# Token-major u, q and k blocks, dense attention in three queued steps, later state-space groups and decay rows sent by DMA, in a two-layer hybrid trunk

## The chip, the cores and the metric

The kernel runs on one core of one Trainium2 chip. The metric is the device time of one execution in microseconds; the time before is the median of three runs. The profile is of one execution. In it TensorE is PE, its weight loads PEld, VectorE DVE, ScalarE ACT, GpSimd POOL, and SyncE, which issues nearly all DMAs, SP.

## What is computed

A trunk of two layers on 256 tokens of width 2048, all in float32, with modulation by a conditioning vector (adaLN). Layer 0 mixes with a spatial-gating MLP (A) beside a state-space scan (B), layer 1 with stick-breaking attention (C, 12 heads of 128) beside dense softmax attention (D, 4 heads; with 256 tokens the block-sparse choice has one block, the token's own). Each layer ends with a SwiGLU FFN. Cut to what the change touches:

```python
# layer 0
u, v, z, xbc, dt_raw = split(hm @ w_in)
v  = layer_norm(gelu(v))                       # in chunks of 128 tokens, heads of 128 columns
mixed = einsum('hts,bcshe->bcthe', tril(w_s), v) + b_s.T[:, :, None]
y_a = gelu(u) * mixed
x, B, C = split(silu(conv(xbc)));  dt = softplus(dt_raw + bias)
a_cum = cumsum(dt * a)                         # per head, in chunks of 128 tokens
y   = (tril(C B^T) * exp(a_cum_t - a_cum_s)) (x dt) + C state exp(a_cum) + d * x
y_b = rms_norm(y * silu(z))
x   = x + gate * (concat(y_a, y_b) @ w_out)
# layer 1
qc, kc, vc, qd, kd, vd = split(hm @ w_in)
y_c = stick_breaking(qc, kc, vc)               # sigmoid weights, cumulated backwards over the keys
y_d = softmax(rms(qd) rms(kd)^T / sqrt(128), causal) vd
x   = x + gate * (concat(y_c, y_d) @ w_out)
```

## The kernel before

**Products.** A weight is taken in slabs of 256 rows by 512 columns (`wslab`, L323): one DMA of 512 KB into `raw` (4 buffers), a cast on ACT to `hi` in fp32r (L331), the rest on DVE to `lo` (L336), 3 buffers each. Every product is three fp32r products: hi by hi, hi by lo, lo by hi. There are two forms of a block of 512 output columns. `dense_ws` (L361) keeps the weight in the array and lets the 256 tokens pass: 8 slabs x 2 x 3 x 4 = 192 matmuls of 256 columns (L379), with the result feature by token. `dense_as` (L399) keeps the activation in the array and lets 512 weight columns pass: 96 matmuls of 512 columns (through `mm`, L163), with the result token by feature. An accumulator takes half of the four PSUM banks of pool psA (2 buffers); everything else uses `pm()`, 4 banks, and smaller tiles with few buffers each (`t2` and `t1` 6, `xc` 3).

**Order.** The program is unrolled, and a list scheduler orders each engine's instructions by priority (place in the program, moved forward by `high_priority`), by its own estimate of time, and by free buffers; each engine then runs its list in that order. `later` holds work that `dense_as` and `dense_ws` issue behind the third slab of the next block (DEFER = 6 k-tiles), `preps` holds steps of which one is issued ahead of each slab, `pump` spreads the adaLN products (L208 on DVE, fed by `araw` DMAs) over the slabs.

**Layer 0.** 14 blocks in ORDER (x, v, z) are made in three passes over k. Then come the 4 u blocks in `dense_ws`, then the output projection in two halves of 4 blocks each: the ya half (k-tiles of y_a), then the yb half (k-tiles of y_b). After u, 16 splits (`split`, L468 to 470) make the pairs of y_a from `vt`, which holds v, then mixed, then y_a, with the columns on partitions after `spatial`. The pairs lie in the same slots (`hslot`) as those of the norm's output that the u blocks read.

**State-space groups.** `ssd_group(g)` works on 4 k-tiles. For each k-tile j it spreads two rows of the cumulated decay over 128 partitions by four small matmuls (identR by `ath` and `atl`, result `bc` in a `pm` bank), makes the decay matrix on ACT (L897, L899, L904) and DVE (L900, L905), multiplies on PE into `py`, and adds on DVE (L913). `ssd_out` then multiplies by z (L971) and sums squares (L498). The four groups stand behind blocks SSD_AT = (12, 14, 16, 18) of the running count: 12 is z2, 14 and 16 are the blocks u0 and u2, 18 is the first block of the ya half. The splits of y_b are L1230 and L1231.

**Layer 1.** vd in `dense_as`, then qd and kd in `dense_ws`; `rstd_of` forms each head's root mean square by a product with ones (8 in all) and L482, L1351. Dense attention runs head by head (L1363 to L1388). Then for each of three groups of four heads: q and k blocks in `dense_ws`, the weights w of the stick-breaking heads (L1401 to 1421, two `t2` tiles and one `pm` bank a head), a v block in `dense_as`, and the products with v (`y_out` splits them, L469 and L470). The output projection takes the k-tiles in the order 12 to 15, then 0 to 11.

Of the kernel before, what the change touches and what calls it, by code (L numbers as in the profile page):

```python
# [8 lines left out]
F32 = mybir.dt.float32  # L9
F32R = mybir.dt.float32r  # L10
# [5 lines left out]
P = 128  # L16
# [34 lines left out]
SSD_AT = (12, 14, 16, 18)  # L51
# [3 lines left out]
def trunk(ctx: ExitStack, tc: tile.TileContext, x, c, norm_mix_g, norm_ffn_g, ada_w, ada_b,  # L55
# [69 lines left out]
    identR = cst.tile([HB, HB], F32R, name="identR")  # L125
    V.tensor_copy(identR, ident[0:HB, 0:HB])
# [4 lines left out]
    def small_loads():  # L131

        for dst, src in ((rows2[0:96, :], ssd_conv_w[0].rearrange("j (k p) -> (j k) p", p=P)),
# [6 lines left out]
                         (rows1[82:83, 0:HB], ssd_d),  # L140
                         (hb[:, 0, :], ssd_dt_bias.partition_broadcast(P)),
# [218 lines left out]

    def dense_ws(w, c0, ks, ahead=W_AHEAD):  # L361
# [38 lines left out]
    def dense_as(w, c0, ks, ahead=W_AHEAD, head=None, tail=False, hold=False):  # L400
# [13 lines left out]
        for pi, part in enumerate(parts):  # L414
# [15 lines left out]
            for n, j, (r, i, x) in order:  # L430
# [5 lines left out]
                bh, bl = run[i][1]  # L436
# [37 lines left out]

    def rstd_of(sqs, scale):

        ps = pm()
        for i, t in enumerate(sqs):
            mm(ps[:, 0:S], ones, t, first=(i == 0), last=(i == len(sqs) - 1))
        r = tmp.tile([P, S], F32, tag="rb", name="rb", bufs=2)  # L480
        A.activation(r, ps[:, 0:S], AF.Sqrt, bias=eps6, scale=scale)
        V.reciprocal(r, r)  # L482
        return r
# [300 lines left out]
    ath = st([HB, S], "ath", F32R)  # L784
    atl = st([HB, S], "atl", F32R)
# [3 lines left out]
    def ssd_dt():  # L789
# [48 lines left out]
        A.activation(ath, psat[0:HB, 0:S], AF.Copy)  # L838
        V.tensor_tensor(atl, psat[0:HB, 0:S], ath.bitcast(F32), op=OP.subtract)
# [3 lines left out]
        V.tensor_copy(dcol, psD[:, 0:KT])  # L843

# [10 lines left out]
    def ssd_group(g):  # L855
# [29 lines left out]
        for j in range(4):  # L885
            kt = 4 * g + j
            bc = pm()
            for i in range(2):
                h = 2 * kt + i
                oh = identR[:, h:h + 1].to_broadcast([HB, P])  # L890
                mm(bc[:, i * S:(i + 1) * S], oh, ath, first=(i == 0), last=False)
                mm(bc[:, i * S:(i + 1) * S], oh, atl, first=False)
# [11 lines left out]
            A.activation(cev, bc.rearrange("p (i t) -> p i t", i=2)[:, :, P:S], AF.Exp)  # L904
            V.tensor_tensor(cev, cev, cT[:, None, P:S].to_broadcast([P, 2, P]), op=OP.mult)  # L905
# [37 lines left out]
    def mix(b, h):  # L943
        return vt[b][:, :, h * P:(h + 1) * P]

    def spatial(b):
# [8 lines left out]
        bs = t2().rearrange("p (h t) -> p h t", h=4)  # L955
        nc.sync.dma_start(bs, gm_b_s[:, 4 * b:4 * b + 4, :].partition_broadcast(P))
        for h2 in range(2):
            ps = pm()
            for i in range(2):
                h = 2 * h2 + i  # L960
                for cc in range(2):
                    o = i * S + cc * P
                    mm(ps[:, o:o + P], mix(b, h)[:, cc, :], w[:, h, :], first=(i == 0 and cc == 0))
            for i in range(2):
                h = 2 * h2 + i
                V.tensor_tensor(mix(b, h), ps[:, i * S:(i + 1) * S].rearrange("p (c t) -> p c t", c=2),
                                bs[:, h, None, :].to_broadcast([P, 2, P]), op=OP.add)
# [39 lines left out]
    rate[0] = RATE  # L1007
    for b in range(4):
# [333 lines left out]
    for c0, gcol in ((QD0, 80), (KD0, 81)):  # L1342
        acc = dense_ws(w_in1, c0, ks1)
        t = b4()
        with tc.high_priority(offset=600):
            A.activation(t, acc, AF.Copy)
# [128 lines left out]
```

## Time and profile before

| | |
|---|---|
| median of 3 runs | 2578.42 us (2578.0 to 2580.18) |
| time of the profiled execution | 2575.71 us |
| its span, first to last instruction | 2574.0 us |
| mean granted TensorE clock | 0.999 |
| PE / PEld / DVE / ACT busy | 99% / 85% / 73% / 49% |
| DMA | 672.96 MB, mean 261 GB/s |

PE is busy for 99% of the span, but matmuls are pipelined and overlap in the records, so the busy share doesn't say how much of it is needed. The chain of work in order of time gives, for each run of matmuls of one kind, its length and its count; their quotient is the spacing of the matmuls, and that is what the engine's time is made of.

### The profile page before, as it was taken

Reading aid. Unit: us, or ns where it says so; the run is one execution under the profiler, and the core shown is the slowest. Engines: PE = TensorE matmul, PEld = TensorE weight load, DVE = VectorE, ACT = ScalarE, POOL = GpSimd, SP = SyncE. Lnnn points to the kernel's source line nnn. Section 1 sums busy time; section 2 is a strip of 40 time slices with the busy share of each in tenths; the row PEclk is TensorE's granted clock in tenths of the full one; section 3 lists DMA queues with packets and bytes.
Section 4 is the critical chain, followed back from the end, with each engine's and each line's share of the span. In section 5 each row is a group of like instructions: output and inputs, shape, how many; then the busy total and the mean of one; then the engine's idle time right before and its main releaser. Section 6 shows DMA issues by size and latency. Waiting matters only on the chain.

```text
span 2574.0 us, 35773 instructions
## 1 busy us (share of the span) xinstructions
PE 2542.3 (99%) x13621; PEld 2184.9 (85%) x13621; DVE 1876.0 (73%) x2027; ACT 1263.5 (49%) x1612; POOL 5.4 (0%) x19
## 2 busy tenths in 40 slices
PE   7999999999999999999999999999999999999999
PEld 6999899988788888888888899998788888888887
DVE  7899887889878888777777787768765455545454
ACT  5535866645645443344444655544744443344443
POOL 0000000000000000000000000000000000000000
PEclk9999999999999999999999999999999999999999
DMA  9999667798799988998998688888686666666655
GB/s 347 313 347 310 196 207 239 259 310 296 266 326 331 312 302 313 322 315 302 307 305 304 216 269 265 257 265 284 196 266 195 190 188 203 199 193 190 188 202 166
DMA packets 307830, 672.96 MB, mean 261 GB/s; under 512 B 24048, under 2 KB 26570, under 8 KB 307658
## 3 DMA queue, kind: packets, MB, share of 16 engines
q1 hardware_dynamic: 307530, 670.66, 79.1%
q8 instruction: 106, 1.74, 0.3%
q14 instruction: 66, 0.54, 0.1%
q10 hardware_dynamic: 128, 0.02, 0.0%
HBM read 668.46 MB, written 2.13 MB: 261 GB/s over the span
## 4 chain that ended last, share of the span: by engine, by line
PE 96%; DVE 1%; ACT 1%; DMA 1%; issue 0%; SPq 0%; ACTq 0%; DVEq 0%
PE accps L163 69%; PE accps L379 19%; PE pm L163 7%; PE pm L154 1%; DVE acc L208 1%; DMA blk<-in_ada_w 0%; DMA raw<-in_ffn_w_gate 0%; DMA t<-in_gm_w_s 0%; PE pm L871 0%; DMA t<-in_gm_ln_b 0%; DVE t L1134 0%; ACT h L1130 0%; DVE xr L1037 0%; ACT t L927 0%; ACT t L1121 0%
## 5 line engine op out<-in xcount | busy, mean ns | idle before, releaser
L331 ACT ACTIVATE hi<-raw 128x1024 fp32r<-128x1024 f32 (+1 forms) x864 | 903.1, 1046 | 1168.8 <-PE accps L163 880.7
L336 DVE TENSOR_TENSOR lo<-raw,hi 128x1024 fp32r<-128x1024 f32 (+1 forms) x864 | 1039.5, 1205 | 566.5 <-ACT hi L331 560.7
L163 PE MATMUL accps<-hi,h 128*128 128x512 f32 x1840 | 498.0, 391 | 0.0
L163 PE MATMUL accps<-lo,h 128*128 128x512 f32 x1840 | 494.6, 390 | 0.0
L163 PE MATMUL accps<-hi,l 128*128 128x512 f32 x1840 | 494.0, 390 | 0.0
L208 DVE SCALAR_TENSOR_TENSOR acc<-araw,ct,acc 128x1024 f32<-128x1024 f32 (+2 forms) x377 | 465.5, 1235 | 3.5 <-DMA araw<-in_ada_w 3.0
L163 PEld LDWEIGHTS accps<-hi,l 128*128 128x128 f32 x1840 | 344.9, 188 | 72.0 <-issue 0.2
L163 PEld LDWEIGHTS accps<-lo,h 128*128 128x128 f32 x1840 | 344.2, 188 | 71.8
L163 PEld LDWEIGHTS accps<-hi,h 128*128 128x128 f32 x1840 | 341.7, 188 | 68.6 <-ACT hi L331 0.2
L379 PE MATMUL accps<-h,hi 128*128 128x256 f32 x1392 | 376.5, 285 | 2.5 <-ACT h L522 1.7
L379 PE MATMUL accps<-h,lo 128*128 128x256 f32 x1392 | 376.1, 285 | 1.3 <-DVE lo L336 1.3
L379 PE MATMUL accps<-l,hi 128*128 128x256 f32 x1392 | 374.6, 285 | 0.0
L163 PE MATMUL accps<-hi,blk 128*128 128x512 f32 x1440 | 357.5, 390 | 0.0
L163 PEld LDWEIGHTS accps<-hi,blk 128*128 128x128 f32 x1440 | 269.5, 188 | 55.6
L379 PEld LDWEIGHTS accps<-h,hi 128*128 128x128 f32 x1392 | 259.3, 192 | 5.3 <-ACT h L522 1.9
L379 PEld LDWEIGHTS accps<-h,lo 128*128 128x128 f32 x1392 | 258.7, 192 | 2.7 <-DVE lo L336 1.5
L379 PEld LDWEIGHTS accps<-l,hi 128*128 128x128 f32 x1392 | 258.8, 192 | 0.8
L163 PE MATMUL accps<-lo,blk 128*128 128x512 f32 x720 | 192.5, 389 | 0.0
L163 PEld LDWEIGHTS accps<-lo,blk 128*128 128x128 f32 x720 | 135.1, 188 | 28.1
L163 PE MATMUL pm<-hi,blk 128*128 128x512 f32 x224 | 57.0, 390 | 0.3 <-ACT hi L331 0.3
L579 DVE TENSOR_TENSOR blk<-accps,blk 128x1024 f32<-128x1024 f32 x40 | 48.7, 1218 | 3.1 <-PE accps L163 2.6
L163 PEld LDWEIGHTS pm<-hi,blk 128*128 128x128 f32 x224 | 42.0, 188 | 9.4 <-ACT hi L331 0.7
(282 smaller groups left out, 1335.8 us busy)
## 6 DMA issues: line engine op xcount, KB each, us to landing
araw<-in_ada_w SPq DMA_DIRECT2D x323, 512.0 KB, 5.6
raw<-in_ffn_w_gate SPq DMA_DIRECT2D x176, 512.0 KB, 4.5
raw<-in_ffn_w_up SPq DMA_DIRECT2D x176, 512.0 KB, 4.4
raw<-in_ffn_w_down SPq DMA_DIRECT2D x176, 512.0 KB, 4.5
raw<-in_ab_w_in SPq DMA_DIRECT2D x128, 512.0 KB, 5.1
raw<-in_cd_w_in SPq DMA_DIRECT2D x96, 512.0 KB, 4.7
raw<-in_ab_w_out SPq DMA_DIRECT2D x64, 512.0 KB, 5.6
raw<-in_cd_w_out SPq DMA_DIRECT2D x32, 512.0 KB, 5.3
```

The costliest lines, as they stand in the source:

```text
L154: return T.transpose(dst, src, ident)
L163: return T.matmul(o, a, b, start=first, stop=last, skip_group_check=True)
L208: V.scalar_tensor_tensor(acc, r, ct[nr][:, g:g + 1], acc, op0=OP.mult, op1=OP.add)
L331: A.activation(hi, raw, AF.Copy)
L336: wlast[1] = V.tensor_tensor(lo, raw, hi.bitcast(F32), op=OP.subtract)
L379: dense_mm[0] = T.matmul(acc[:, n, :], a[:, n * P:(n + 1) * P], b, start=first and n % 2 == 0, stop=final, skip_group_check=True)
L579: V.tensor_tensor(dst, acc, dst, op=OP.add)
```

## The change

The 4 u blocks and the 8 q and k blocks go from `dense_ws` to `dense_as`. For y_a, `spatial` now writes token by feature with its bias from a column, gelu(u) is multiplied whole, and `turn` transposes y_a per pair of k-tiles (4 transposes and 2 splits), queued ahead of slabs of u2, u3 and the first ya block. For q and k, `turned` queues a `flip` (8 transposes) behind the third slab of the next block; the stick-breaking weights and the products with v are queued in the same way, so that they come later by about three slabs. The squares of qd and kd are summed on ACT in the token form. Dense attention is split in `moba_probs`, `moba_turn` and `moba_out`, two heads a step, one step ahead of a slab. The groups of the state-space scan stand behind blocks 12, 14, 18 and 20. The cumulated decay goes to DRAM once, and a broadcast DMA of 256 KB (`decay`) brings the two rows of each k-tile to all partitions, two k-tiles ahead.

```diff
-SSD_AT = (12, 14, 16, 18)
+SSD_AT = (12, 14, 18, 20)
...
+    def turn(j, src, make):
+        with tc.high_priority(offset=600):
+            ps = pm()
+            with tc.issue_after(dense_mm[0].ins):
+                for i in range(2):
+                    for cc in range(2):
+                        o = ((2 * j + i) % 4) * P
+                        transpose(ps[:, i * S + cc * P:i * S + (cc + 1) * P], src[:, cc, o:o + P])
+            for i in range(2):
+                make(2 * j + i, ps[:, i * S:(i + 1) * S])
+
+    def queue_turns(js, src, make, skip=0):
+        preps.extend([lambda: None] * skip)
+        for j in js:
+            preps.append(lambda j=j: turn(j, src[j // 2], make))
...
-        A.activation(ath, psat[0:HB, 0:S], AF.Copy)
-        V.tensor_tensor(atl, psat[0:HB, 0:S], ath.bitcast(F32), op=OP.subtract)
+        rows = t1()[0:HB, :]
+        A.activation(rows, psat[0:HB, 0:S], AF.Copy)
+        nc.sync.dma_start(decay_rows, rows)
+        for kt in range(2):
+            decay(kt)
...
+    def decay(kt):
+        if kt < KT:
+            d = decays[kt] = tmp.tile([P, 512], F32, tag="bc", name="bc", bufs=2)
+            nc.sync.dma_start(d, decay_rows[2 * kt:2 * kt + 2, :].rearrange("h t -> (h t)").partition_broadcast(P))
...
-            bc = pm()
-            for i in range(2):
-                h = 2 * kt + i
-                oh = identR[:, h:h + 1].to_broadcast([HB, P])
-                mm(bc[:, i * S:(i + 1) * S], oh, ath, first=(i == 0), last=False)
-                mm(bc[:, i * S:(i + 1) * S], oh, atl, first=False)
+            bc = decays.pop(kt)
...
             A.activation(cev, bc.rearrange("p (i t) -> p i t", i=2)[:, :, P:S], AF.Exp)
+            decay(kt + 2)
...
-        bs = t2().rearrange("p (h t) -> p h t", h=4)
-        nc.sync.dma_start(bs, gm_b_s[:, 4 * b:4 * b + 4, :].partition_broadcast(P))
-        for h2 in range(2):
...
+        for cc in range(2):
             ps = pm()
+            for h in range(4):
+                c = slice(h * P, (h + 1) * P)
+                mm(ps[:, c], w[:, h, :], vt[b][:, cc, c], first=h == 0)
+            V.tensor_tensor(vt[b][:, cc, :].rearrange("p (h e) -> p h e", h=4), ps.rearrange("p (h e) -> p h e", h=4),
+                            cols[1][:, 4 * b:4 * b + 4, None].to_broadcast([P, 4, P]), op=OP.add)
...
+    def make_a(k, ps):
+        ya[k] = hslot(k)
+        split(ya[k], ps)
+
     for b in range(4):
-        acc = dense_ws(w_in0, 512 * b, ksm)
+        if b >= 2:
+            queue_turns(range(4) if b == 2 else range(4, 6), vt, make_a, 4)
+        acc = dense_as(w_in0, 512 * b, ksm)
         finish0(14 + b)
         with tc.high_priority(offset=600):
-            A.activation(acc, acc, AF.Gelu_apprx_tanh)
-            for h in range(4):
-                V.tensor_tensor(mix(b, h), acc[:, h, :].rearrange("p (c t) -> p c t", c=2), mix(b, h), op=OP.mult)
+            u = tb()
+            A.activation(u, acc, AF.Gelu_apprx_tanh)
+            V.tensor_tensor(vt[b], u, vt[b], op=OP.mult)
...
-    ya = []
-    for k in range(KT):
-        h = hslot(k)
-        split([t.rearrange("p (c t) -> p c t", c=2) for t in h], mix(k // 4, k % 4))
-        ya.append(h)
+    queue_turns(range(6, 8), vt, make_a, 2)
...
+    def block(c0, scale=1.0):
+        acc = dense_as(w_in1, c0, ks1)
+        t = tb()
         with tc.high_priority(offset=600):
+            A.activation(t, acc, AF.Copy, scale=scale)
+        return t
+
+    def turned(t, into, scale=1.0):
+        def use(j, ps):
+            if j == 0:
+                into.append(b4())
+            A.activation(into[0][:, 2 * j:2 * j + 2, :], ps, AF.Copy, scale=scale)
+        later.append(lambda: flip(t, use))
...
-        acc = dense_ws(w_in1, c0, ks1)
...
-            rb = rstd_of([sq], 1.0 / P)
-            V.scalar_tensor_tensor(t[:, h, :], t[:, h, :], cols[1][:, gcol:gcol + 1], rb, op0=OP.mult, op1=OP.mult)
+        t = block(c0)
+        th = t.rearrange("p c (h e) -> p c h e", h=4)
+        sq = small(8, "sq").rearrange("p (c h) -> p c h", c=2)
+        for cc in range(2):
+            for h in range(4):
+                A.activation(t1()[:, 0:P], th[:, cc, h, :], AF.Square, accum_out=sq[:, cc, h:h + 1])
+        A.activation(sq, sq, AF.Sqrt, bias=eps6, scale=1.0 / P)
+        V.reciprocal(sq, sq)
+        V.tensor_tensor(th, th, sq[:, :, :, None].to_broadcast([P, 2, 4, P]), op=OP.mult)
+        turned(t, into, cols[1][:, gcol:gcol + 1])
...
+    preps.extend([lambda: None] * 5)
+    for step_of in (moba_probs, moba_turn, moba_out):
+        preps.extend(lambda h=h, f=step_of: [f(h), f(h + 1)] for h in (0, 2))
+        preps.append(lambda: None)
...
+    for g in range(3):
+        qT, kT, ws = [], [], []
+        turned(block(QC0 + 512 * g, SCALE), qT)
+        turned(block(KC0 + 512 * g), kT)
+        later.append(lambda qT=qT, kT=kT, ws=ws: weights(qT, kT, ws))
+        vc = v_block(VC0 + 512 * g)
+        later.append(lambda g=g, ws=ws, vc=vc: weighted(g, ws, vc))
```

## Rows read from the trace of the kernel before

**Rows 1.** The page: the busy shares, the granted clock in 40 slices, and the chain that ended last, by engine and by line (the first of its long line is what is read).

```profile
PE 2542.3 (99%) x13621; PEld 2184.9 (85%) x13621; DVE 1876.0 (73%) x2027; ACT 1263.5 (49%) x1612; POOL 5.4 (0%) x19
PEclk9999999999999999999999999999999999999999
PE 96%; DVE 1%; ACT 1%; DMA 1%; issue 0%; SPq 0%; ACTq 0%; DVEq 0%
```

**Rows 2.** The waits of PE over the whole run, longest first: who waited for whom, us in total, times, longest.

```profile
PE pm L163 <- DVE t L614: 6.4, 1, 6.4
...
PE pm L951 <- DMA t<-in_gm_w_s: 1.6, 1, 1.6
PE pm L163 <- DVE t L900: 1.4, 1, 1.4
PE accps L379 <- DVE lo L336: 1.3, 1, 1.3
```

**Rows 3.** The chain in order of time (start, length, what, how many): two runs of `dense_ws`, then two `dense_as` blocks of the FFN and the flip of 8 transposes behind them, then one step of 4 transposes in the norm ahead of the FFN.

```profile
177.06 31.30 PE accps L379 x261
...
1687.53 26.39 PE accps L379 x220
...
1149.10 43.55 PE accps L163 x192
1192.64 0.87 PE pm L154 x8
...
807.99 0.44 PE pm L154 x4
```

**Rows 4.** Groups of PE instructions by line, tiles and shape: the small matmuls that spread the decay, those with ones in `rstd_of`, and the transposes of `flip` (busy us, mean ns of one, idle before).

```profile
L163 PE MATMUL pm<-ath,identR 32*128 32x256 f32 x32 | 9.9, 328 | 0.0
L163 PE MATMUL pm<-atl,identR 32*128 32x256 f32 x32 | 8.2, 275 | 0.0
L163 PE MATMUL pm<-t,ones 128*128 128x256 f32 x16 | 4.4, 379 | 0.0
L154 PE MATMUL pm<-ident,blk 128*128 128x128 f32 x176 | 22.8, 272 | 0.0
```

**Rows 5.** PE in order of time behind the qd block: products with ones among dense matmuls (four of the former, of two records each, and three of the latter up to the last row).

```profile
1485.48 0.60 PE L163 MATMUL pm<-t,ones 128*128 128x256 f32 x2
...
1486.58 1.03 PE L163 MATMUL pm<-t,ones 128*128 128x256 f32 x4
...
1487.56 0.28 PE L379 MATMUL accps<-h,hi 128*128 128x256 f32 x1
```

**Rows 6.** The chain in order of time from the first ya block on: dense runs (L163 of accps) and, between them, the pieces of the last two state-space groups.

```profile
500.23 10.00 PE accps L163 x44
...
511.96 9.52 PE accps L163 x41
...
523.57 11.14 PE accps L163 x49
...
543.75 1.53 PE pm L163 x6
...
554.09 1.73 PE pm L163 x16
...
576.58 1.73 PE pm L163 x16
...
587.83 1.08 PE pm L163 x12
```

**Rows 7.** DVE in the stretch 530 to 612 us: the last group's instructions, the residuals of the ya blocks and the splits of y_b (count: shortest, median and longest ns, first and last start).

```profile
L900 DVE TENSOR_TENSOR t<-t,cbm x4: 681/684/685, 549.3 to 582.6; 128x512 f32<-128x512 f32 x4
L913 DVE SCALAR_TENSOR_TENSOR blk<-blk,dcol,pm x4: 470/475/481, 558.0 to 592.7; 128x256 f32<-128x256 f32 x4
L971 DVE TENSOR_TENSOR blk<-blk x1: 1215/1215/1215, 597.3 to 597.3; 128x1024 f32<-128x1024 f32 x1
L1231 DVE SCALAR_TENSOR_TENSOR l<-blk,cols,h x16: 473/476/508, 585.5 to 609.6; 128x256 fp32r<-128x256 f32 x16
```

**Rows 8.** The u blocks, the ya half and the yb half of layer 0: length, busy time of PE, PEld, DVE, ACT and POOL, granted clock, DMA share, GB/s.

```profile
385.00:500.00 115.00, 114.97 (x951) 109.44 (x950) 96.80 (x129) 70.58 (x119) 0.00 (x0) 1.00 0.79 248
500.00:590.00 90.00, 90.00 (x451) 72.69 (x451) 80.83 (x96) 49.55 (x82) 1.28 (x4) 1.00 0.86 291
590.00:690.00 100.00, 100.00 (x452) 82.94 (x450) 89.97 (x104) 51.23 (x70) 2.49 (x3) 1.00 0.93 321
```

**Rows 9.** The last stick-breaking group in layer 1: the copy of its k block, the last exponential of each head, the splits behind the product with v, and the chain at the first block of the output projection.

```profile
L1400 ACT ACTIVATE blk<-accps x1: 1009/1009/1009, 1714.8 to 1714.8; 128x1024 f32<-128x1024 f32 x1
...
L1418 ACT ACTIVATE t<-pm x4: 474/494/495, 1729.3 to 1760.1; 128x384 f32<-128x384 f32 x4
...
L470 DVE TENSOR_TENSOR blk<-pm,blk x4: 416/418/425, 1749.1 to 1765.5; 128x256 fp32r<-128x256 f32 x4
...
1765.08 7.05 PE accps L163 x31
```

**Rows 10.** DMA issues (size, median us to landing): a slab, the bias of the spatial mix that is spread over all partitions; and what SP's queue waited for (us in total, times, longest).

```profile
raw<-in_ab_w_in SPq DMA_DIRECT2D x128, 512.0 KB, 5.1
t<-in_gm_b_s SPq DMA_DIRECT2D x4, 256.0 KB, 4.8
...
SPq L325 <- DVE lo L336: 1363.3, 776, 9.0
```

More of the change, by code (lines that the diff above doesn't have):

```diff
@@ L473, in trunk @@
     xr = res.tile([P, 2, D], F32, name="xr")
[L475 to L483, printed above, removed]
     class Ssq:
@@ L1212, in queue @@
                 preps.append(lambda j=j: self.pair(j, paced))
-    ya = []
-    for k in range(KT):
-        h = hslot(k)
-        split([t.rearrange("p (c t) -> p c t", c=2) for t in h], mix(k // 4, k % 4))
-        ya.append(h)
+    queue_turns(range(6, 8), vt, make_a, 2)
     for b in range(4):
         g = gate_tile(0, 2, b)
-        acc = dense_as(w_out0, 512 * b, [(k, ya[k]) for k in range(KT)])
+        acc = dense_as(w_out0, 512 * b, [(k, lambda k=k: ya[k]) for k in range(KT)])
         finish0(18 + b)
@@ L1360, in y_out, with moba_probs @@
         split((yh[:, k % 4, :], yl[:, k % 4, :]), ps)
-    qd, kd = qk_d
-    for h in range(4):
+    probs = {}
+    def moba_probs(h):
+        q, k = qd[0][:, h, :], kd[0][:, h, :]
         ps = pm()
-        mm(ps[:, 0:P], qd[:, h, 0:P], kd[:, h, 0:P])
-        mm(ps[:, P:384], qd[:, h, P:S], kd[:, h, :], first=False)
-        s = t2()
+        mm(ps[:, 0:P], q[:, 0:P], k[:, 0:P])
+        mm(ps[:, P:384], q[:, P:S], k, first=False)
+        s = probs[h] = t2()
         V.scalar_tensor_tensor(s[:, 0:384], ps[:, 0:384], SCALE, cmask, op0=OP.mult, op1=OP.add)
@@ L1387, in trunk, with weights @@
         y_out(12 + h, ps[:, 0:S])
-    with tc.issue_after(last_exp.ins):
-        both_sets = A.preload_act_table_set("natural_log_exp_and_others")
-    pb = past[:, None, :].to_broadcast([P, 2, P])
-    for g in range(3):
-        acc = dense_ws(w_in1, QC0 + 512 * g, ks1)
-        qT = b4()
-        with tc.high_priority(offset=600):
-            A.activation(qT, acc, AF.Copy, scale=SCALE)
-        acc = dense_ws(w_in1, KC0 + 512 * g, ks1)
-        kT = b4()
-        with tc.high_priority(offset=600):
-            A.activation(kT, acc, AF.Copy)
-        ws = []
+    both_sets = []
+    preps.extend([lambda: None] * 5)
+    for step_of in (moba_probs, moba_turn, moba_out):
+        preps.extend(lambda h=h, f=step_of: [f(h), f(h + 1)] for h in (0, 2))
+        preps.append(lambda: None)
+    pb = past[:, None, :].to_broadcast([P, 2, P])
+    def weights(qT, kT, ws):
         for h in range(4):
+            q, k = qT[0][:, h, :], kT[0][:, h, :]
             ps = pm()
-            mm(ps[:, 0:S], kT[:, h, 0:P], qT[:, h, :], last=False)
-            mm(ps[:, S:384], kT[:, h, P:S], qT[:, h, P:S], first=False, last=False)
+            mm(ps[:, 0:S], k[:, 0:P], q, last=False)
+            mm(ps[:, S:384], k[:, P:S], q[:, P:S], first=False, last=False)
             sp = t2()
-            with tc.issue_after(both_sets.ins):
+            with tc.issue_after(both_sets[0].ins):
                 A.activation(sp[:, 0:384], ps[:, 0:384], AF.Abs)
@@ L1436, in trunk @@
         g = gate_tile(1, 2, b)
-        acc = dense_as(w_out1, 512 * b, [(k, ypair(k)) for k in korder], tail=b == 3, hold=b == 3)
+        acc = dense_as(w_out1, 512 * b, [(k, lambda k=k: ypair(k)) for k in korder], tail=b == 3, hold=b == 3)
         with tc.high_priority(offset=600):
```

44 lines of the change are left out of this document (16 added, 28 removed).

## The prediction

> **What bounds the kernel now.** I read the page first. PE is busy for 99% of the span at full granted clock, and 96% of the chain that ended last is PE's [rows 1]. A busy PE can hide slack, so next I read PE's waits: the long ones belong to the start, and behind it a handful of 1.3 to 1.6 us is all there is [rows 2]. So PE hardly ever waits, and the time is the number of matmuls times their spacing. The chain in order of time gives the spacing. `dense_ws`: 31.30 us for 261 and 26.39 us for 220, both 119.9 ns a matmul. `dense_as`: 43.55 us for 192, 226.8 ns [rows 3]. The records themselves last longer (390 ns in one form), because they overlap; they are not used. What the change is worth is thus the PE work that it takes out and puts in, plus any new wait of PE.
>
> **Term 1, twelve blocks change their form.** A `dense_ws` block is 192 x 119.9 ns = 23.02 us, a `dense_as` block 96 x 226.8 ns = 21.78 us [rows 3]. The difference is 1.25 us, times 12 (4 u, 8 q and k): -15.0 us. All of it lies on PE, so on the path.
>
> Here a rule speaks against the change. The Trainium skill (TensorE: Matmul & The Clock Gate, section Back-to-back issue gap) gives N/2.4 + 2.5 ns for a warm matmul of N columns, which is 109.2 ns and 215.8 ns. By it a block would gain 0.25 us and term 1 would be -3 us. The trace differs: both spacings are 11 ns longer [rows 3], a cost per matmul, and `dense_ws` pays it twice as often.
>
> **Term 2, the decay rows leave PE.** 64 small matmuls go, four for each of 16 k-tiles [rows 4]. Where a piece of the chain holds the products of one k-tile with the next one's four, it takes 1.73 us, and without them (the last) 1.08 us [rows 6]: 0.65 us. Part of that is the change-over between kinds of matmul, which the products still pay: four matmuls of 256 columns at the dense spacing of 119.9 ns are 0.48 us. I take 0.45 us and get -7.2 us; the other end is 0.65 x 16 = -10.4 us.
>
> **Term 3, rstd_of goes.** Eight products with ones are two records each [rows 4]. From 1485.48 to 1487.56 us four of them stand beside three dense matmuls: 2.08 - 3 x 0.12 = 1.72 us, 0.43 us each [rows 5]. -3.4 us.
>
> **Term 4, transposes come in.** A flip of 8 takes 0.87 us and a step of 4 takes 0.44 us in the chain, 109 ns a transpose [rows 3]. Eight flips for q and k are +7.0 us, eight turns for y_a +3.5 us. The dense-attention products, the transposes of the probabilities and the spatial products keep their number and size, so they cost nothing new on PE; ordering them in three steps has no PE wait to remove, since none stands there [rows 2].
>
> Terms 1 to 4 sum to -15.0 - 7.2 - 3.4 + 10.5 = -15.1 us.
>
> **Term 5, waits that go.** PE lost 1.4 us to L900, DVE behind a decay matrix that came late, 1.6 us to the load of the spatial weights, and 1.3 us to a split that came late in the same stretch [rows 2]. With the decay rows in SBUF before ACT needs them, and without the broadcast load of the bias, some of this goes. I take -1.5 us, between 0 and -4.3 us.
>
> **Term 6, waits that come.** Four places.
>
> (a) The last group now stands behind the third ya block. Counting 96 matmuls a block from 500.23 us, ya0 ends near 526, ya2 near 578.5 and ya3 near 602 us [rows 6]. Before, this group stood behind ya0 and its last split of y_b started at 609.6 us [rows 7], 84 us later. After the change, yb0 needs the group's k-tiles at its seventh slab: ya3 (21.8 us), six slabs (6 x 2.72 us) and the group's own PE pieces (some 6.4 us) are 44.5 us. It fits only if the group gets faster. It should: its k-tiles followed each other every 10 to 11 us, because the four matmuls for the next k-tile ran on PE together with the products of this one (the 1.73 us pieces at 554.09 and 576.58 us [rows 6]), so ACT could not start the next before. With the rows sent by DMA ACT goes ahead, and the group is bound by its DVE work. That is four times L900 and L913 (0.68 + 0.48 us [rows 7]) and L905 (much like L913), then L971 and three scalings and four sums of like size, some 11.5 us. Of a slab's 2.72 us the split takes 1.2 us, so 1.5 us is left, if it goes before the adaLN products: 11.5 / 1.5 x 2.72 = 21 us. With some 10 us for hops between the engines and 4 us for the last splits it is 35 us (estimates from these rows). Cost 0, with 10 us to spare. DVE is busy for 84 to 90% of this stretch [rows 8], but with work that may wait.
>
> (b) The turns queued in u2 split into slots that u3 still reads. So up to four of them hold the four `pm` banks from the second half of u2 into the first half of u3, about 11 us. Group 1 waits for a bank; the dense blocks use none, and y_b is needed 100 us later. Cost 0.
>
> (c) Each decay load waits on SP until ACT has read the k-tile two before, with slab loads and `araw` loads queued behind it. SP waits for buffers most of the time anyway, up to 9.0 us, and PE loses nothing by that [rows 10, 2]; a load of 256 KB of this kind lands in 4.8 us [rows 10]. 12 more such loads than before, 3.1 MB, find the DMA engines at 79% in the u blocks and 86% in the ya half [rows 8]. Cost 0, up to 5 us (two slabs) if two come late.
>
> (d) In layer 1 the last group's weights now start behind the third slab of the v block and a flip, 9 us later than now. Now the copy of k at 1714.8 us leads to the last split at 1765.5 us, and the chain of the output projection runs on at 1765.08 us [rows 9]: no slack is left in the order as it is. PE can take slabs of the next block meanwhile, but there are three slab buffers, so about two slabs, 5.4 us. Cost between 0 and 9 us; I take 2.5.
>
> **Sum.** 2575.7 (the profiled execution) - 15.1 - 1.5 + 2.5 = 2561.6 us. The median of the runs lies 2.7 us above that execution, so 2564 us is the forecast, -0.55%.
>
> **Rivals.** First, *the last group comes late*. If it still takes 84 us behind its block, yb0's seventh slab is late by 39.5 us; PE can fill 5.4 us of it with the next block's slabs. 34 us lost against -16.6 us won is +17.5: 2596 us, slower. It decides against the change from about 44.5 + 5.4 + 16.6 = 66 us on. For it: DVE is at 90% in the yb half [rows 8], and the group's steps before were that slow [rows 7]. Against it: they were slow through a hop over PE that goes.
>
> Second, *attention or SP costs more than I take*: (c) or (d) at their upper ends adds 6 us or so: 2570 us. For it: (d) has no slack. Against it: the scheduler fills PE with other slabs, and does so now without a wait [rows 2].
>
> Third, *more is won*: term 2 at 10.4 us, term 5 at 4.3 us, nothing for (d), together 8.5 us more: 2556 us.
>
> Fourth, *the form is worth nothing*: if a block of either kind is bound by something else once it stands here (DVE's splits at 84% in the u blocks [rows 8], say), term 1 falls to some -3 us: 2576 us. The rule on the issue gap above gives the same time. The 192 in a row at 226.8 ns [rows 3] speak against it.
>
> Fifth, *transposes cost their record*, not their spacing: 272 ns [rows 4] for 96 is +26.1 instead of +10.5 us: 2580 us, no change. The Trainium skill (the same page, section Part 4: PE-mode transpose) reckons about 275 ns for one inside a kernel and says that the fast clock does not engage for them. The record agrees with that figure, but here eight of them cost the chain 0.87 us, and the granted clock stays at 1.00 [rows 3, 1].
>
> **How the numbers follow.** Forecast 0.60, attention or SP 0.15, more won 0.12, last group late 0.05, form worth nothing 0.04, transposes 0.04. The range from 2555 to 2573 holds the forecast with its bounds and the second and third rival, and leaves out the rest, 0.13. A measurement of this kernel can tell about 0.2% (5.2 us) from no change: faster 0.87 (the first three), same 0.08, slower 0.05.
>
> **What would show it.** In the chain the u, q and k blocks must stand as runs of L163 at 226.8 ns; no matmuls on identR or of t by ones; flips of 0.87 us and turns of 0.44 us beside them. In the last group, L897 of all four k-tiles should come without a product between, and the last L1231 within 45 us of ya2's end. PE's waits should show nothing above 3 us behind the start. A wait of PE for y_b's splits at yb0, or for y_out's splits at the first block of layer 1's output projection, would make the prediction wrong, and so would spacings other than these.

## The result, and the profile after

| | before | after |
|---|---|---|
| median, 5 runs each | 2578.0 us (2577.49 to 2580.18) | 2565.29 us (2564.17 to 2565.73) |
| ratio to before | | 0.995 [0.9936, 0.9964] |
| time and span of the profiled execution | 2575.71, 2574.0 us | 2565.73, 2563.9 us |
| DMA | 672.96 MB | 676.01 MB |

The change makes the kernel 0.5% faster. The forecast was 2564 us. Read in the order of the prediction, the page comes first, with its busy line and its two lines on the chain [rows 1].

```profile
PE 2528.8 (99%) x12485; PEld 2128.0 (83%) x12485; DVE 1862.2 (73%) x1993; ACT 1265.6 (49%) x1640; POOL 6.5 (0%) x19
...
PE 96%; DVE 1%; DMA 1%; ACT 1%; issue 0%; SPq 0%; DVEq 0%; ACTq 0%
```

PE has 1136 matmuls less and is as busy as before. DMA has 1% of the chain, as before. The waits of PE over the whole run show one wait for DMA that has grown [rows 2]:

```profile
PE pm L162 <- DVE t L621: 6.8, 1, 6.8
...
PE pm L960 <- DMA t<-in_gm_w_s: 3.6, 2, 2.3
PE accps L396 <- DVE lo L335: 3.1, 2, 2.4
PE pm L162 <- DVE acc L207: 2.6, 1, 2.6
```

The 1.4 us of L900 are gone. But PE loses 3.6 us to the spatial weights (1.6 before) and 3.1 us to late splits (1.3 before). The chain in order of time shows the changed blocks [rows 3]: first a turn of y_a, then in layer 1 a flip and a whole block.

```profile
458.81 0.44 PE pm L153 x4
...
1489.77 0.87 PE pm L153 x8
1490.65 21.78 PE accps L162 x96
```

21.78 us for 96 is 226.9 ns a matmul, and nothing stands between flip and block. The transposes have grown from 176 to 272 in the group of `flip` and `turn`, at the same mean record [rows 4]:

```profile
L153 PE MATMUL pm<-ident,blk 128*128 128x128 f32 x272 | 35.7, 272 | 0.0
```

The last state-space group: its four decay matrices on DVE, then its product with z and the splits of y_b [rows 7], then its products in the chain [rows 6].

```profile
L911 DVE TENSOR_TENSOR t<-t,cbm x4: 683/686/686, 564.2 to 573.7; 128x512 f32<-128x512 f32 x4
```

```profile
L1238 DVE SCALAR_TENSOR_TENSOR l<-blk,cols,h x16: 471/474/510, 581.2 to 604.8; 128x256 fp32r<-128x256 f32 x16
...
L974 DVE TENSOR_TENSOR blk<-blk x2: 1214/1216/1219, 543.3 to 589.9; 128x1024 f32<-128x1024 f32 x2
```

```profile
574.51 2.12 PE pm L162 x28
576.62 4.54 PE accps L162 x19
581.16 1.07 PE pm L162 x12
582.23 40.12 PE accps L162 x176
```

Four decay matrices within 10 us, where they took 33 us before, and 40 us of dense matmuls in one piece behind them.

**Where the time went.** To split the span I charged each matmul with the undisturbed spacing of its kind (119.9, 226.8 or 109 ns, and so on) and called the rest of its distance to the next one lost. The table holds these worked-out sums in us, lost time by stretch (small stretches are left out), for all the kernels below. The last column is the part of the lost time that falls where the granted clock was 0.50; in after, around 341 us, dense matmuls of 256 columns follow each other every 213 ns there. Each row is one execution, the profiled one.

| kernel | PE work | lost in 0–150 | 300–400 | 500–550 | 550–700 | 1500–1800 | lost in all | of it at clock 0.50 |
|---|---|---|---|---|---|---|---|---|
| before | 2519.8 | 24.6 | 5.7 | 0.5 | 3.3 | 0.6 | 44.0 | 1.6 |
| **after** | 2504.2 | 28.1 | 9.6 | 0.1 | 3.6 | 1.1 | 49.6 | 6.1 |
| before_groups_late | 2519.8 | 24.9 | 5.8 | 0.8 | 4.9 | 1.6 | 46.3 | 0.0 |
| after_groups_early | 2504.2 | 26.0 | 8.1 | 5.0 | 3.2 | 1.1 | 52.4 | 6.1 |
| after_decay_on_pe | 2511.9 | 28.4 | 3.3 | 0.8 | 5.1 | 1.2 | 48.9 | 4.6 |
| after_spatial_early | 2504.2 | 28.3 | 6.7 | 0.1 | 3.6 | 1.1 | 46.5 | 4.3 |
| after_start_filled | 2504.7 | 24.1 | 9.5 | 0.1 | 3.6 | 1.1 | 44.8 | 1.5 |
| before_start_gap | 2519.6 | 23.8 | 5.9 | 0.5 | 3.3 | 0.6 | 43.7 | 1.6 |
| after_uqk_ws | 2508.0 | 24.7 | 4.3 | 0.4 | 3.6 | 0.4 | 40.1 | 1.5 |
| after_flips_twice | 2511.2 | 27.8 | 9.7 | 0.1 | 3.6 | 1.1 | 49.5 | 6.1 |
| after_heads_serial | 2504.2 | 25.9 | 7.5 | 0.1 | 3.6 | 12.2 | 56.3 | 8.2 |
| after_decay_on_act | 2504.2 | 28.3 | 7.8 | 0.1 | 3.6 | 1.1 | 48.2 | 4.6 |
| after_uws_filled | 2506.2 | 24.4 | 4.3 | 0.4 | 3.6 | 1.1 | 40.6 | 0.0 |
| after_uws_filled_early | 2506.2 | 26.1 | 6.7 | 0.5 | 3.6 | 1.1 | 45.1 | 4.1 |

Work fell by 15.6 us, lost time grew by 5.6 us, and the span fell by 10.1 us. Two stretches hold the growth: the start (+3.5) and 300 to 400 us (+3.9). By the last column 4.5 us of the growth lie where the clock was 0.50, and 1.1 us elsewhere. The start in windows of 5 us (columns: length, busy time of PE, PEld, DVE, ACT, POOL, granted clock, DMA share, GB/s):

```profile
30.00:35.00 5.00, 2.15 (x7) 0.80 (x6) 4.88 (x5) 1.22 (x2) 0.00 (x0) 0.97 0.94 365
35.00:40.00 5.00, 5.00 (x25) 5.00 (x25) 2.48 (x10) 1.97 (x4) 0.00 (x0) 0.50 0.42 117
40.00:45.00 5.00, 5.00 (x38) 5.00 (x37) 4.58 (x8) 4.72 (x8) 0.00 (x0) 0.85 0.81 241
```

Before, all three had a granted clock of 1.00. After, PE stood idle for 2.6 us ahead of the sums of the modulation (1.1 us before), and behind that came a stretch at 0.50, the lower of the two levels (1.2 GHz). The same happens from 338.5 us on, where PE had just waited three times, up to 2.4 us, for spatial weights and splits. After, then the same stretch before:

```profile
338.50:341.80 3.30, 3.30 (x17) 3.30 (x17) 3.30 (x6) 0.97 (x3) 0.00 (x0) 0.50 0.63 179
```

```profile
338.50:341.80 3.30, 3.30 (x30) 3.30 (x29) 3.30 (x9) 1.52 (x2) 0.00 (x0) 1.00 0.81 246
```

There is a third one near 123 us; the kernel before has one alone, near 119 us. They come and go within one and the same kernel: in the 52 runs of the kernel before that stand beside the experiments, the mean granted clock lies between 0.996 and 1.000. The ten at 1.000 have a median of 2576.1 us, the twenty at 0.998 or less one of 2579.9 us. The five runs of the changed kernel lie at 0.997 and 0.998.

### The profile page after: what moved, and what is told of

Read it like the earlier page. It is cut to its first block, busy times and chain, and to the rows that moved or that the text cites. A ratio compares the mean times of both kernels' runs of the same rounds, so it can differ in the third digit from the quotient of the medians.

```text
span 2563.9 us, 33519 instructions
## 1 busy us (share of the span) xinstructions
PE 2528.8 (99%) x12485; PEld 2128.0 (83%) x12485; DVE 1862.2 (73%) x1993; ACT 1265.6 (49%) x1640; POOL 6.5 (0%) x19
## 2 busy tenths in 40 slices
DMA packets 309630, 676.01 MB, mean 264 GB/s; under 512 B 24272, under 2 KB 26842, under 8 KB 309466
## 3 DMA queue, kind: packets, MB, share of 16 engines
q8 instruction: 98, 1.61, 0.2%
## 4 chain that ended last, share of the span: by engine, by line
PE 96%; DVE 1%; DMA 1%; ACT 1%; issue 0%; SPq 0%; DVEq 0%; ACTq 0%
PE accps L162 79%; PE accps L396 8%; PE pm L162 6%; PE pm L153 2%; DMA t<-in_gm_w_s 1%; DVE acc L207 0%; DMA blk<-in_ada_w 0%; ACT hi L330 0%; DVE lo L335 0%; DMA raw<-in_ffn_w_gate 0%; DVE t L867 0%; PE pm L887 0%; ACT t L939 0%; DVE t L1145 0%; ACT h L1141 0%
## 5 line engine op out<-in xcount | busy, mean ns | idle before, releaser
L162 PE MATMUL accps<-hi,h 128*128 128x512 f32 x2224 | 603.8, 392 | 0.0
L162 PE MATMUL accps<-lo,h 128*128 128x512 f32 x2224 | 600.4, 391 | 0.0
L162 PE MATMUL accps<-hi,l 128*128 128x512 f32 x2224 | 599.9, 390 | 0.0
L162 PEld LDWEIGHTS accps<-hi,l 128*128 128x128 f32 x2224 | 416.5, 188 | 87.1 <-issue 0.8
L396 PE MATMUL accps<-h,lo 128*128 128x256 f32 x624 | 164.0, 287 | 3.1 <-DVE lo L335 3.1
L396 PE MATMUL accps<-h,hi 128*128 128x256 f32 x624 | 163.7, 286 | 2.3 <-ACT h L529 1.7
L396 PE MATMUL accps<-l,hi 128*128 128x256 f32 x624 | 163.2, 286 | 0.4 <-DVE l L530 0.4
L396 PEld LDWEIGHTS accps<-h,hi 128*128 128x128 f32 x624 | 115.2, 193 | 4.5 <-ACT h L529 1.9
L396 PEld LDWEIGHTS accps<-h,lo 128*128 128x128 f32 x624 | 114.7, 194 | 4.7 <-DVE lo L335 3.5
L396 PEld LDWEIGHTS accps<-l,hi 128*128 128x128 f32 x624 | 115.0, 195 | 0.8 <-DVE l L530 0.6
```

What stands on the lines that cost most here:

```text
L162: return T.matmul(o, a, b, start=first, stop=last, skip_group_check=True)
L396: dense_mm[0] = T.matmul(acc[:, n, :], a[:, n * P:(n + 1) * P], b, start=first and n % 2 == 0, stop=final, skip_group_check=True)
```

## Experiments

Ratios are to the kernel before, whose median in the three sets of runs was 2577.3, 2577.99 and 2578.21 us. Diffs are against the kernel that the name begins with. The changed kernel was not run again beside the experiments: "slower than after" compares with its median above. A trace is one execution and can lie some us from the median of its runs, which is said where it matters.

**1. The group order alone, in the kernel before.**

```diff
-SSD_AT = (12, 14, 16, 18)
+SSD_AT = (12, 14, 18, 20)
```

> The kernel before, with the state-space groups moved alone (behind blocks 12, 14, 18, 20). Theory (a group is long because each k-tile's decay rows go over PE): group 3 keeps its 50 to 60 us, so its y_b comes late for yb0, PE waits there 10 us or more, and the time is 2588 us or more, slower than before. Rival (the order of the groups is itself a part of the gain, or nothing): PE does not wait at yb0 and the time is 2575 to 2580 us.

2579.34 us, 1.0008 [0.9999, 1.0016]. The last group was late, as the theory had it, yet PE hardly noticed: the rival was right. Splits of y_b on DVE, then the chain behind 619 us:

```profile
L1231 DVE SCALAR_TENSOR_TENSOR l<-blk,cols,h x16: 477/480/482, 579.8 to 632.6; 128x256 fp32r<-128x256 f32 x16
```

```profile
619.38 1.07 ACT hi L331
...
626.66 1.07 ACT hi L331
```

The block yb0 began at 597.1 us, so its seventh slab was due at 613.4 us (six slabs of 2.72 us). The last split came 19 us later, and 550 to 700 us lost 1.6 us more than before. PE ran slabs of the next block, and even those waited for ACT's casts, not for y_b. So the prediction's look-ahead of two slabs (5.4 us) was wrong, and the point of 66 us from which its first rival decides was too early.

**2. The group order alone, taken back.** SSD_AT = (12, 14, 16, 18) in the changed kernel.

> The changed kernel, with the groups back behind blocks 12, 14, 16, 18. Theory: PE's work is the same, and the groups are short now, so the place is worth little: 2562 to 2569 us. Rival (the move carries the gain): 2572 us or more.

2571.93 us, 0.9975 [0.9965, 0.9985]: 6.6 us slower than after by the medians, at the edge of the rival's range and out of the theory's (the profiled execution, 2568.43 us, is one of the two fastest of nine). PE's waits from 480 to 560 us hold one line, which the changed kernel doesn't have:

```profile
PE accps L162 <- ACT h L486: 4.6, 2, 3.4
```

The group behind u2 and the turns of y_a want the same four `pm` banks. With it there, the turns of k-tiles 8 to 11 came only when it had ended, and the splits behind them (L486) between 510 and 515 us, where after has them near 485 to 491 us. Moving the groups is worth 5 us of lost time, 1.6 us of it at the clock of 0.50 that follows the wait. In the kernel before, which has no turns, it is worth nothing (experiment 1). That the banks set this order is read from the code, not tested.

**3. The decay rows by matmuls again.**

```diff
-            bc = decays.pop(kt)
+            bc = pm()
+            for i in range(2):
+                h = 2 * kt + i
+                oh = identR[:, h:h + 1].to_broadcast([HB, P])
+                mm(bc[:, i * S:(i + 1) * S], oh, ath, first=(i == 0), last=False)
+                mm(bc[:, i * S:(i + 1) * S], oh, atl, first=False)
...
-            decay(kt + 2)
```

> The changed kernel, with the decay rows spread on PE again by the 64 small matmuls, all else as changed. Theory: PE's work grows by 7.2 us (6.4 to 10.4), and each group takes 45 to 60 us again instead of 23 to 35, so that the last comes late for yb0 and PE waits there some 10 us: 2578 to 2590 us. Rival (the transfers save PE's work only): 2571 to 2576 us, the groups as short as in the changed kernel.

2570.27 us, 0.9969 [0.9957, 0.998], 5.0 us slower than after and just under the rival's range; PE's work grew by 7.7 us. A group takes 52 to 58 us again, as the theory had it, from its first transposes to its product with z, against 23 to 35 us with the transfers (read from the start times). But as in experiment 1 the late y_b cost only 1.5 us. 300 to 400 us went from 9.6 to 3.3 us lost, 1.5 us of it by the clock, which stayed at 1.00 there. So the transfers are worth the PE work that they take out, less some 6 us of waits in that stretch.

**4. The spatial weights loaded ahead.** Cut: `spatial_load` issues the same DMA some blocks earlier, into two buffers of the gate tiles.

```diff
-        wraw = t2().rearrange("p (h s) -> p h s", h=4)
-        nc.sync.dma_start(wraw, gm_w_s[0, 4 * b:4 * b + 4].rearrange("h t s -> t h s"))
+        wraw = wraws.pop(b)
...
+        if i in (6, 8):
+            spatial_load(i // 2 - 3)
```

> The changed kernel, with the loads of the spatial weights issued some blocks ahead, into two buffers of the gate tiles that are free until the output projection. Theory (the 9.6 us that PE loses between 300 and 400 us come from these loads, with DVE standing in line behind a product that waits for them): 4 to 7 us less, 2558 to 2561 us. Rival (DVE's convolutions and norm are late in any case): 2564 to 2567 us.

2564.74 us, 0.9945 [0.9932, 0.9957]: within the runs' scatter of after, as the rival said. The wait for the load is gone, but the splits are still late, and a wait at 120 us has grown, for an operand that ACT makes from the modulation:

```profile
PE accps L396 <- DVE lo L335: 3.5, 3, 2.2
PE accps L396 <- ACT h L529: 2.9, 1, 2.9
```

The late splits stand behind another load: DVE waits for the gain of the layer norm, and the chain from 318 to 342 us runs over two of its loads, where after's runs over two of the spatial weights (4.43 and 3.45 us):

```profile
320.58 4.14 DMA t<-in_gm_ln_g
...
326.26 3.74 DMA t<-in_gm_ln_g
```

No run brings that load forward.

**5 and 6. The idle stretch at the start, filled in after and widened in before.** Ahead of the sums PE multiplies some blocks by the identity into a bank that nobody reads; only how many is changed.

```diff
-            for t in firsts[10:]:
+            for t in firsts[10:] + firsts[-1:] * 2:
```

```diff
-            for t in firsts[10:]:
+            for t in firsts[10:-1]:
```

> The changed kernel with the last of the identity products that nobody reads (pm from blk and ident, ahead of the sums of the modulation) done three times instead of once: two more pairs of 128x512 float32 matmuls, 1.12 us a pair, in TensorE's idle stretch of 2.63 us ahead of the sums at 34.53 us. The output is the same. Theory: the granted clock of 0.50 between 35 and 40 us in the changed kernel comes from that idle stretch (1.12 us in the kernel before, clock 1.00), so with the stretch filled the clock stays at 1.00 through 30 to 50 us and the span is 2 to 4 us shorter: 2561 to 2563.5 us. Rival: the clock falls there for another reason (the transfers run at 406 GB/s instead of 387 in that stretch), stays near 0.5, and the time stays at 2564 to 2567 us.

> The kernel before with one of those pairs of identity products left out, the last one, so that TensorE is idle some 1.3 us longer ahead of the sums (about 2.5 us instead of 1.12). The output is the same. Theory: the granted clock falls below 1.00 between 30 and 45 us, to near 0.5 in 35:40, as in the changed kernel, and the time is 2 to 3.5 us longer than the kernel before, with nothing else of the change in it. Rival: the clock stays at 1.00 in every stretch and the time is that of the kernel before within 1.5 us.

The filled one: 2562.06 us, 0.9939 [0.9926, 0.9951], 3.2 us less than after. The widened one: 2578.34 us, 1.0001 [0.9992, 1.001]. Windows of the filled one, then of the widened one:

```profile
30.00:35.00 5.00, 4.30 (x13) 1.72 (x13) 4.86 (x5) 1.23 (x2) 0.00 (x0) 1.00 0.97 376
35.00:40.00 5.00, 4.96 (x42) 4.75 (x42) 3.64 (x12) 3.49 (x7) 0.00 (x0) 1.00 0.55 144
```

```profile
30.00:35.00 5.00, 2.35 (x10) 0.95 (x8) 4.72 (x5) 1.26 (x2) 0.00 (x0) 1.00 1.06 379
35.00:40.00 5.00, 5.00 (x32) 5.00 (x31) 3.42 (x11) 3.08 (x6) 0.00 (x0) 0.66 0.73 219
```

So the theory holds for the clock: the idle stretch brings it down, in a kernel that has nothing else of the change, and filling it keeps it up (one kernel below, after_uqk_ws, kept 1.00 all the same). For the time it holds only in the filled one; in the widened one the rival was right. In the widened one PE lost 1.3 us more in the first 50 us and 2.2 us less from 100 to 150 us: the stretch at 0.50 near 119 us, which cost the kernel before 1.6 us, didn't come in this execution, so the time stayed the same. In the filled one neither the stretch at 35 us (3.1 us) nor the one at 123 us (1.5 us) came, and the lost time of the first 150 us fell by 4.0 us. So nearly all of the gain is the clock's, and the runs bear it out: all five of the filled kernel have a mean clock of 0.999. Why the later stretch went with the first one stays open.

**7. Ten blocks back in `dense_ws`** (u, and q and k of the stick-breaking heads).

```diff
-        acc = dense_as(w_in0, 512 * b, ksm)
+        acc = dense_ws(w_in0, 512 * b, ksm)
...
-        turned(block(QC0 + 512 * g, SCALE), qT)
-        turned(block(KC0 + 512 * g), kT)
+        for c0, into, scale in ((QC0, qT, SCALE), (KC0, kT, 1.0)):
+            acc = dense_ws(w_in1, c0 + 512 * g, ks1)
```

> The changed kernel with ten of its twelve changed blocks (four of u, six of the dense attention's q and k) back in the old form: weights as the stationary operand, and no transposes behind them; the group order, the decay sums by transfer, the three steps and the last two blocks stay. Theory: each block costs 23.02 us again instead of 21.78, ten times 1.24 is +12.4 us, and 80 transposes at 109 ns go, -8.7 us: +3.7 us net, 2567 to 2571 us. Rival: the form itself is worth nothing (216 ns for a 512-column matmul as for two of 256 columns), so only the transposes count: 2555 to 2559 us. Second rival: each transpose costs its record of 272 ns, -21.8 us: also about 2556 us, but with the blocks' spacing in the chain different in the two forms.

(The expectation calls the six blocks the dense attention's; the edit takes those of the stick-breaking heads. With u the spatial mix, its bias by DMA and its splits go back to their old form too, which the cut leaves out.) 2564.3 us, 0.9944 [0.9932, 0.9957]. The work rose by 3.8 us, against +3.7 expected; since the work is counted with these spacings, that alone is no test of them. The test is the spacing in the chain. A run of the old form:

```profile
431.25 45.66 PE accps L396 x379
```

120.5 ns a matmul. By the rule of the Trainium skill that the prediction weighed (TensorE: Matmul & The Clock Gate, Back-to-back issue gap, where it stands for an isolated matmul) ten blocks differ by 2.5 us, not 12.4, and the work would have fallen by 6.2 us; the spacings of both forms speak against it. The time was 1.0 us less than after's, in no range that was given. The trace is of the fastest of five runs (2559.79 us, 4.5 us under their median). In it lost time fell by 9.5 us: 3.4 in the first 150 us, where the clock stayed at 1.00, and 5.3 from 300 to 400 us. At the median about half of that is not there; the run at 2559.79 us has a mean clock of 0.999, the slowest (2566.29 us) one of 0.997.

**8. Each of the 64 transposes of q and k done twice.**

```diff
-                    transpose(ps[:, i * S + cc * P:i * S + (cc + 1) * P], src[:, cc, n * P:(n + 1) * P])
+                    for _ in range(times):
+                        transpose(ps[:, i * S + cc * P:i * S + (cc + 1) * P], src[:, cc, n * P:(n + 1) * P])
```

> The changed kernel with each of the 64 transposes that turn the eight q and k blocks done twice into the same place. The output is the same. Theory: a transpose takes 109 ns of TensorE's time between neighbours, so 64 more take +7.0 us, all of it on the path: 2570 to 2574 us. Rival: each takes its record's 272 ns, +17.4 us: 2580 to 2585 us. Second rival: they fall into waits that TensorE has anyway: under +3 us.

2571.72 us, 0.9974 [0.9963, 0.9984]: +6.4 us by the medians, +6.9 us by the spans, against +7.0 expected.

```profile
1489.94 1.75 PE pm L153 x16
1491.69 21.78 PE accps L162 x96
```

109 ns each, all on the path: both traces lost 6.1 us at the clock of 0.50, so their spans can be compared. The rival with 272 ns is out.

**9. The u blocks alone back in `dense_ws`, with the filled start.** Diffs of 7 (its first part) and 5.

> The changed kernel with the identity products of after_start_filled and with the four blocks of u alone back in the old form (weights stationary, the spatial mix and its splits as before); q and k blocks, groups, decay sums and the three steps stay. The output is the same. Theory: what uqk_ws won came from u: its four blocks cost 4 x 1.24 = 5.0 us more and 32 transposes of 109 ns less (3.5 us), but the waits of TensorE between 300 and 400 us (gm_w_s and lo, 6.7 us in the changed kernel, 3.4 in uqk_ws) are cut by half or more, 5 us by the spacing: 3 us less than after_start_filled (2562.1), so 2557 to 2560.5 us. Rival: uqk_ws was faster only by its start (clock 1.00 there by chance) and by its q and k blocks; then u costs its +1.5 us: 2562.5 to 2565 us.

2560.11 us, 0.9927 [0.9913, 0.9941]: the theory's time, and the fastest version here, 5.2 us under after. Against the filled start alone it is 2.0 us less by the medians, whose intervals overlap, and 2.9 us less by the spans, where 1.5 us are a stretch at 0.50 that only after_start_filled has. PE's work is 1.5 us more than in after_start_filled, as expected; 300 to 400 us lost 4.3 us instead of 9.5.

```profile
PE accps L396 <- DVE lo L335: 3.1, 2, 1.7
PE pm L963 <- DMA t<-in_gm_w_s: 1.6, 1, 1.6
```

So no gain of the new form of u is left here: its 1.5 us net go under in waits. The form of q and k saves work: between this kernel and after_uqk_ws the work differs by 2.3 us if the 0.5 us of filling is set aside. No run shows its worth in time by itself.

**10. The same with the spatial weights loaded ahead.** Diffs of 9 and 4.

> after_uws_filled with the loads of gm_w_s issued ahead of time into buffers of their own, as in after_spatial_early. The output is the same. Theory: the remaining wait for gm_w_s (1.8 us) goes and one or two of the waits for lo stay: 1 to 2.5 us less than after_uws_filled. Rival: VectorE is as late as the load, the wait only changes its name: within 1 us of after_uws_filled.

2562.5 us, 0.9936 [0.9923, 0.9949]: 2.4 us more by the medians, which neither theory nor rival had; the intervals overlap, the runs don't. The wait for the weights is gone, but 100 to 150 us lost 5.4 us instead of 2.5, and 300 to 400 us lost 6.7 instead of 4.3. The two traces are the slowest and the fastest of their five runs, and 4.1 of the 4.5 us between them lie at a clock of 0.50, near 122 and 334 us. The chain ahead of the first of these:

```profile
114.55 6.14 DMA araw<-in_ada_w
```

It is an adaLN load, for which PE waits through DVE. In experiment 4 such a load holds 4.48 us of the chain at 120 us. Two of the early loads go out at 28.5 us, ahead of other adaLN loads; that this is why one is late 86 us on isn't shown.

**11. Dense attention head by head**, each head in one step.

```diff
-    for step_of in (moba_probs, moba_turn, moba_out):
-        preps.extend(lambda h=h, f=step_of: [f(h), f(h + 1)] for h in (0, 2))
-        preps.append(lambda: None)
+    preps.extend(lambda h=h: [moba_probs(h), moba_turn(h), moba_out(h)] for h in range(4))
```

> The changed kernel with the dense attention's four heads done one after the other, each in one preparation step (scores, turns, products together) instead of three steps of two heads each. The output is the same. Theory: the three steps are worth little, because TensorE's wait at 1450 us (1.0 us in the kernel before) went with the sums of squares, not with the steps: within 2 us of the changed kernel, 2563.5 to 2567.5 us. Rival: without the steps TensorE waits at each head for the exponentials and the copies, four times 1 to 2 us: 2569 to 2574 us.

2573.88 us, 0.9983 [0.9974, 0.9992]: 8.6 us slower than after. The rival was right, though not as it told it: it is one wait, not four. PE's waits, then windows:

```profile
PE pm L1412 <- DVE t L1403: 4.7, 1, 4.7
```

```profile
1560.00:1570.00 10.00, 7.08 (x35) 5.60 (x33) 7.55 (x10) 3.18 (x5) 0.00 (x0) 1.00 0.84 284
1570.00:1580.00 10.00, 6.89 (x26) 5.85 (x27) 1.24 (x5) 6.92 (x13) 0.00 (x0) 0.62 0.22 77
1580.00:1590.00 10.00, 10.00 (x44) 8.35 (x44) 4.32 (x5) 3.87 (x6) 0.00 (x0) 0.87 0.35 99
```

PE runs its list in order, and in this list a head's transposes stand right behind its scores. Where the dense slabs between them are used up, PE waits through mask, maximum, exponential and scaling, and the clock falls behind the idle stretch: 11 us are lost in that stretch, 5.2 of them at the clock of 0.50 (the start and 300 to 400 us lost 4 us less than in after, so the spans differ by 6.7 us and the medians by 8.6).

**12. The decay transfers on ScalarE's queue.**

```diff
-        nc.sync.dma_start(decay_rows, rows)
+        nc.scalar.dma_start(decay_rows, rows)
...
-            nc.sync.dma_start(d, decay_rows[2 * kt:2 * kt + 2, :].rearrange("h t -> (h t)").partition_broadcast(P))
+            nc.scalar.dma_start(d, decay_rows[2 * kt:2 * kt + 2, :].rearrange("h t -> (h t)").partition_broadcast(P))
```

> The changed kernel with the store of the decay rows and their sixteen loads issued from ScalarE's queue instead of SyncE's. The output is the same. Theory: the seventeen transfers cost their place in SyncE's queue, where the loads of gm_w_s and of weights stand behind them; on another queue the waits between 300 and 400 us fall from 6.7 us towards those of after_decay_on_pe (1.8), and the time is 3 to 6 us less: 2559 to 2562.5 us. Rival: SyncE's queue is not what delays them (the order of VectorE's work is), the waits stay above 5 us, and ScalarE is held up now: 2565 to 2569 us.

2564.1 us, 0.9942 [0.9928, 0.9956], not to be told from after, so nothing shows that ScalarE was held up. The waits from 300 to 400 us are those of after within 0.3 us:

```profile
PE pm L960 <- DMA t<-in_gm_w_s: 3.3, 2, 2.4
PE accps L396 <- DVE lo L335: 3.1, 2, 2.4
```

The theory that the transfers' place in SyncE's queue delays the spatial weights falls.

## Why the prediction was right, and where its sizes were off

**Terms 1 to 4** were forecast at -15.1 us and came out at -15.6 us of PE work, counted with the spacings of the traces. Term 4 is confirmed in the time by its own run (8). For term 1 both spacings stand in the chain (226.9 ns here, 120.5 ns in 7), but no run changes the form alone and shows it in the time. For term 2 experiment 3 counts 7.7 us against 7.2. Term 3 had no run of its own. The fourth and the fifth rival are out: the spacing held in every block, and a transpose costs 109 ns.

**Term 5** is where the step failed. I expected a gain of 1.5 us, since the wait for L900 would go. It went, but the two other waits of the same stretch, which I had thought would shrink, grew to 6.7 us: the spatial stage came out 3.9 us worse, not 1.5 better. The two totals, 3.6 and 3.1 us, also pass the 3 us that the prediction named as a sign, though no single wait is over 2.4 us. Of the 3.9 us, 1.5 are the stretch at the clock of 0.50 behind these waits. The rest depends on two parts of the change: taking back the transfers (3) or the form of u (7, 9) each removes more than half. SyncE's queue isn't it (12). The load of the spatial weights isn't it alone: with it moved ahead 2.9 us went (4), but the loads of the norm's gain then took its place in the chain, and with u in the old form nothing went (10). The loads of the gain and the order of DVE's list are the candidates left, and no run tests them. The figure itself moves by 2 us between kernels whose code up to there is the same (7.5 in experiment 11, 9.7 in 8).

**Term 6.** (a) cost nothing, as forecast, and the group took 34.8 us from its first transposes to its product with z, against an estimate of 35 us. Its start I had wrong: PE took it 17 us before the end of ya2 (555.1 against 572.4 us), so the last split came 32 us behind that block's end. (b) cost nothing, as the group had moved away from the turns; with the old order it costs 5 us (2), a price that the prediction didn't see as this move's gain. For (c) no cost shows on SyncE's queue (12). (d) was forecast at 2.5 us and cost nothing that can be seen. The last split of layer 1 starts at 1767.8 us, and the chain from 1690 to 1790 us is PE alone [rows 9]. Its end:

```profile
1765.21 0.65 PE pm L162 x4
1765.86 24.27 PE accps L162 x107
```

The two-slab look-ahead on which (d) and the first rival rested is the wrong step there (1). "No wait to remove" was right for the three steps, but they are what keeps 8.6 us from coming (11).

**Not foreseen** at all was the clock. The prediction took it as full throughout and has no term for it. At 0.50 the changed kernel lost 6.1 us and the kernel before 1.6 us, most of the difference at the start, where filling the idle stretch took it away (5).

**The sum.** On the profiled execution I forecast 2561.6 us and 2565.7 us came: 0.5 us more work saved, but lost time grew by 5.6 instead of 1.0 us. Without the time lost at 0.50 it grew by 1.1 us, but that is luck too: term 5 was too good and (d) too bad. The median lay 0.4 us below the profiled execution, not 2.7 above, which gave back 3.1 us: the trace of the kernel before is of one of its faster executions, that of the changed kernel the slowest of five runs within 1.6 us. So the close hit (2564 against 2565.3) is partly errors that cancel; sign and size rest on the PE work, which was right.

## What to carry to other kernels

Where an engine is busy for 99%, price a change by the spacing of its instructions in the chain: forecast and count differ here by 0.5 us in 15. Then look at the granted clock in every stretch that holds a wait: here waits of about 2 us were followed by 1.5 to 3 us more, lost at the lower clock. Waits that a change moves around are as large as its small gains, so try its parts one by one: undoing the u blocks cost nothing and came out 2 us faster, with intervals that overlap, though their form saves work. A step that is safe alone (turns, groups, head-wise attention) can compete for banks or stand in line with another that is new.

## What was not expected of the hardware

**The clock behind short idle stretches.** Over the kernels of this study the idle time of PE ahead of the sums of the modulation and the granted clock from 35 to 40 us were: up to 1.21 us, always 1.00 (five kernels); 1.61 us, 0.52 (after_decay_on_pe); 2.19 to 2.77 us, 0.50 to 0.66 (seven kernels), but once 1.00 at 2.26 us (after_uqk_ws). So the length of the stretch alone doesn't settle it, and what else does stays open.

**The rate of the first transfers.** From 10 to 30 us the changed kernel moves 406 to 408 GB/s and the kernel before 378 to 387, with much the same loads in that stretch. All variants with the decay rows in DRAM show the higher rate (404 to 408), all without them the lower (378 to 390, after_decay_on_pe among them). The faster arrival fits PE's running out of identity products sooner, at 31.9 us in after and at 33.1 us before; no run changed the rate alone. Why a tensor in DRAM that is first written at 278 us should change it wasn't tried.
